# Interleaving two tensors: the opening half tile in four strided loads

## The chip, the cores and the metric

One Trainium2 chip, one core. The time is that of the device in microseconds, of one execution of the program; a kernel is run several times and the median is given. The profile is of one execution, and its span goes from the first to the last instruction.

## The reference

```python
def setup_inputs():
    batch, seq, dim = 32, 256, 1024
    return {
        "x": np.random.randn(batch, seq, dim).astype(np.float32),
        "y": np.random.randn(batch, seq, dim).astype(np.float32),
    }

def reference(x, y):
    result = np.zeros((batch, seq, dim * 2), dtype=np.float32)
    result[..., 0::2] = x
    result[..., 1::2] = y
```

Two fp32 tensors of 33.6 MB each are woven element by element into one of 67.1 MB. There is no arithmetic. 134.2 MB go through the core's transfers, half of it in and half of it out.

## The kernel before

Each input is taken as one flat row of numbers and cut into n = 8 tiles of 128 partitions x W = 8192 fp32 (4 MB, 32 KB a partition). There are two buffers each for x (`xt`), y (`yt`) and the output (`ot`). A tile of x and one of y give two output halves (h = 0, 1), each of 128 x 8192 elements: VectorE copies 4096 elements a partition of x into the even places of `ot[h]` (L70) and 4096 of y into the odd places (L73). So each output half is one transfer of 4 MB.

Three engines share the work, each with a program of its own, held together by semaphores alone:

- SP issues the loads. For each tile k it issues x (L55) and then y (L58). From tile 2 on it first waits on the semaphore `woven`, which VectorE raises after each copy, until the buffer is free. All of SP's transfers go through one queue.
- VectorE runs the copies in order: x into half 0, y into half 0, x into half 1, y into half 1. It waits for the x tile (`xsem`, L65), for the store that last used the output buffer (`osem`, L69), and for the y tile (`ysem`, L72).
- ACT issues the stores (L80) when `woven` says that a half is complete. The very first half is stored in two parts (2048 and 6144 columns). ACT's transfers go through a second queue.

The opening is special. The first x tile is loaded in two halves of 4096 columns: the first by SP (L46, `xsem[0]`), the second by ACT (L49, `hsem`). Between them in the program stands a tiny transfer of ACT (L48, `tsem`) that copies 16 x 128 elements from x to the output; the right values are stored over it later, and ACT waits for it before its first store. Every transfer raises its semaphore by 16 when it has landed, so a wait for one of them is a wait for 16.

A program begins with an opening block in which the engines meet at a barrier: each drains its work, signals, and goes on when all have. `tile_interleave_kernel` moves the first transfer of SP (L46) and the first of ACT (L48) out of the body and into that opening block, just ahead of each engine's drain, so that they are issued before the barrier (L101 to L119). All else, the second x half (L49) and the first y tile (L58) included, is issued after it.

Of the kernel before, what the change touches and what calls it, by code (L numbers as in the profile page):

```python
# [3 lines left out]


def _interleave(nc, x, y, out):
    P = 128
    W = 8192
    H = W // 2  # L10

    total = 1
    for s in x.shape:
        total *= s
    n = total // (P * W)
    assert n * P * W == total

    def rows(ap, names, k):
        flat = ap.rearrange("b s d -> (b s d)")
        return flat[k * names : (k + 1) * names].rearrange("(p w) -> p w", p=P)  # L20

    fp32 = mybir.dt.float32
    xt = [nc.alloc_sbuf_tensor(f"xt{b}", [P, W], fp32).ap() for b in (0, 1)]
    yt = [nc.alloc_sbuf_tensor(f"yt{b}", [P, W], fp32).ap() for b in (0, 1)]
    ot = [nc.alloc_sbuf_tensor(f"ot{b}", [P, W], fp32).ap() for b in (0, 1)]

    xsem = [nc.alloc_semaphore(f"xsem{b}") for b in (0, 1)]
    hsem = nc.alloc_semaphore("hsem")
    tsem = nc.alloc_semaphore("tsem")
    ysem = [nc.alloc_semaphore(f"ysem{b}") for b in (0, 1)]  # L30
    woven = nc.alloc_semaphore("woven")
    osem = [nc.alloc_semaphore(f"osem{b}") for b in (0, 1)]

    xs = [rows(x, P * W, k) for k in range(n)]
    ys = [rows(y, P * W, k) for k in range(n)]
    os_ = [rows(out, 2 * P * W, k) for k in range(n)]

    Q = W // 4

    def parts(k, h):  # L40
        return [slice(0, W)] if k or h else [slice(0, Q), slice(Q, W)]

    def stored(k, h):
        return 16 * sum(len(parts(j, h)) for j in range(k))

    nc.sync.dma_start(out=xt[0][:, :H], in_=xs[0][:, :H]).then_inc(xsem[0], 16)  # L46
    few = (slice(0, P, P // 16), slice(0, 128))
    nc.scalar.dma_start(out=os_[0][few], in_=xs[0][few]).then_inc(tsem, 16)  # L48
    nc.scalar.dma_start(out=xt[0][:, H:], in_=xs[0][:, H:]).then_inc(hsem, 16)  # L49
    for k in range(n):  # L50
        b = k % 2
        if k >= 2:
            nc.sync.wait_ge(woven, 4 * (k - 2) + 3)
        if k:
            nc.sync.dma_start(out=xt[b], in_=xs[k]).then_inc(xsem[b], 16)  # L55
        if k >= 2:
            nc.sync.wait_ge(woven, 4 * (k - 2) + 4)
        nc.sync.dma_start(out=yt[b], in_=ys[k]).then_inc(ysem[b], 16)  # L58

    for k in range(n):  # L60
        b = k % 2
        for h in (0, 1):
            c = slice(h * H, (h + 1) * H)
            if h == 0:
                nc.vector.wait_ge(xsem[b], 16 * (k // 2 + 1))  # L65
            elif k == 0:
                nc.vector.wait_ge(hsem, 16)
            if k:
                nc.vector.wait_ge(osem[h], stored(k, h))  # L69
            nc.vector.tensor_copy(out=ot[h][:, 0::2], in_=xt[b][:, c]).then_inc(woven, 1)  # L70
            if h == 0:
                nc.vector.wait_ge(ysem[b], 16 * (k // 2 + 1))  # L72
            nc.vector.tensor_copy(out=ot[h][:, 1::2], in_=yt[b][:, c]).then_inc(woven, 1)  # L73

    nc.scalar.wait_ge(tsem, 16)
    for k in range(n):
        for h in (0, 1):
            nc.scalar.wait_ge(woven, 4 * k + 2 * h + 2)
            for c in parts(k, h):
                nc.scalar.dma_start(  # L80
                    out=os_[k][:, h * W : (h + 1) * W][:, c], in_=ot[h][:, c]
                ).then_inc(osem[h], 16)

    nc.scalar.wait_ge(osem[0], stored(n, 0))
    used = sorted(s.num for s in [*xsem, hsem, tsem, *ysem, woven, osem[0]])
    assert used == list(range(used[0], used[-1] + 1)), used
    nc.scalar.sem_clear(range(used[0], used[-1] + 1))
    nc.sync.nop(nofuse=True).wait_op(osem[1], stored(n, 1), "sem-ge").then_inc(
        osem[1], -stored(n, 1)
    )  # L90


def kernel(tc, x, y, out):
    nc = tc.nc
    tc.close()
    tc.compile()

    _interleave(nc, x, y, out)

    blocks = nc.main_func.blocks  # L100
    for engine in (mybir.EngineType.SP, mybir.EngineType.Activation):  # L101
        opening = blocks[0].instructions
        at, moved = next(
            (b, i)
            for b in blocks[1:]
            for i in b.instructions
            if i.engine == engine and i.opcode == "DMACopy"
        )
        assert not (moved.sync_info and moved.sync_info.on_wait)
        body = at.instructions  # L110
        body.remove(moved)
        gate = next(
            n
            for n, i in enumerate(opening)
            if i.engine == engine and i.opcode == "Drain"
        )
        opening.insert(gate, moved)
        at.instructions = body
        blocks[0].instructions = opening  # L119


# [1 line left out]
_INS = ['x', 'y']  # L123
_OUTS = [((32, 256, 2048), 'float32')]


# [23 lines left out]
```

## Time and profile before

| what | value |
|---|---|
| median of 3 runs | 314.29 us (314.17 to 314.34) |
| profiled execution, its own time | 314.17 us |
| its span | 312.8 us |
| bytes read, written | 67.12 MB, 67.12 MB |
| VectorE busy | 72.0 us in 32 copies of 2.29 us |
| chain that ended last | DMA 82%, DVE 12% |

The chain that ended last is followed back from the last instruction; it says which work each step waited for. Here nearly all of it is transfers: VectorE's waits sum up to 206.4 us for stores to leave the output buffers, 11.1 us for the first y tile and 8.6 us for the first half of x. SP waited 217.9 us in six waits for buffers to come free. The issues and how long each took from issue to landing (columns: names, queue, kind, count, size of one, median us to landing):

```profile
out_dram<-ot ACTq DMA_DIRECT2D x15, 4096.0 KB, 34.1
yt<-in_y_dram SPq DMA_DIRECT2D x8, 4096.0 KB, 41.5
xt<-in_x_dram SPq DMA_DIRECT2D x7, 4096.0 KB, 24.3
out_dram<-ot ACTq DMA_DIRECT2D x1, 3072.0 KB, 32.7
xt<-in_x_dram SPq DMA_DIRECT2D x1, 2048.0 KB, 8.6
xt<-in_x_dram ACTq DMA_DIRECT2D x1, 2048.0 KB, 17.5
out_dram<-ot ACTq DMA_DIRECT2D x1, 1024.0 KB, 16.2
out_dram<-in_x_dram ACTq DMA_DIRECT2D x1, 8.0 KB, 6.0
```

A time to landing is long because transfers share the same 16 DMA engines and wait behind one another. 4 MB at the mean rate of 429 GB/s is 9.8 us of all 16 engines.

### The profile page before, as it was taken

Reading aid. Unit: us, or ns where it says so; the run is one execution under the profiler, and the core shown is the slowest. Engines: PE = TensorE matmul, PEld = TensorE weight load, DVE = VectorE, ACT = ScalarE, POOL = GpSimd, SP = SyncE. Lnnn points to the kernel's source line nnn. Section 1 sums busy time; section 2 is a strip of 40 time slices with the busy share of each in tenths; the row PEclk is TensorE's granted clock in tenths of the full one; section 3 lists DMA queues with packets and bytes.
Section 4 is the critical chain, followed back from the end, with each engine's and each line's share of the span. In section 5 each row is a group of like instructions: output and inputs, shape, how many; then the busy total and the mean of one; then the engine's idle time right before and its main releaser. Section 6 shows DMA issues by size and latency. Waiting matters only on the chain.

```text
span 312.8 us, 116 instructions
## 1 busy us (share of the span) xinstructions
DVE 72.0 (23%) x32; POOL 0.2 (0%) x4
## 2 busy tenths in 40 slices
DVE  0216000501405023050230503205032050415410
POOL 0000000000000000000000000000000000000000
DMA  8999999999999999999999999999999999999998
GB/s 336 436 436 436 436 402 432 440 457 415 448 423 427 444 402 469 402 469 402 469 402 465 406 448 423 427 444 402 469 402 469 402 469 402 465 406 448 423 432 373
DMA packets 4928, 134.23 MB, mean 429 GB/s; under 512 B 560, under 2 KB 576, under 8 KB 576
## 3 DMA queue, kind: packets, MB, share of 16 engines
q10 hardware_dynamic: 2624, 69.22, 51.3%
q1 hardware_dynamic: 2304, 65.01, 48.5%
HBM read 67.12 MB, written 67.12 MB: 429 GB/s over the span
## 4 chain that ended last, share of the span: by engine, by line
DMA 82%; DVE 12%; issue 0%
DMA out_dram<-ot 76%; DVE ot L73 6%; DMA yt<-in_y_dram 6%; DVE ot L70 6%
## 5 line engine op out<-in xcount | busy, mean ns | idle before, releaser
L70 DVE COPY ot<-xt 128x4096 f32<-128x4096 f32 x16 | 36.7, 2295 | 215.0 <-DMA out_dram<-ot 206.4
L73 DVE COPY ot<-yt 128x4096 f32<-128x4096 f32 x16 | 36.6, 2288 | 11.1 <-DMA yt<-in_y_dram 11.1
L134 POOL MEMSET const-bfloat16-1.0<- 128x1 bf16 x1 | 0.1, 101 | 0.0
L134 POOL MEMSET const-uint8-127<- 128x1 uint8 x1 | 0.1, 101 | 0.0
L134 POOL MEMSET const-float32-0.0<- 128x1 f32 x1 | 0.1, 98 | 0.2 <-issue 0.2
L134 POOL MEMSET const-float32-1.0<- 128x1 f32 x1 | 0.1, 98 | 0.0
## 6 DMA issues: line engine op xcount, KB each, us to landing
out_dram<-ot ACTq DMA_DIRECT2D x15, 4096.0 KB, 34.1
yt<-in_y_dram SPq DMA_DIRECT2D x8, 4096.0 KB, 41.5
xt<-in_x_dram SPq DMA_DIRECT2D x7, 4096.0 KB, 24.3
out_dram<-ot ACTq DMA_DIRECT2D x1, 3072.0 KB, 32.7
xt<-in_x_dram SPq DMA_DIRECT2D x1, 2048.0 KB, 8.6
xt<-in_x_dram ACTq DMA_DIRECT2D x1, 2048.0 KB, 17.5
out_dram<-ot ACTq DMA_DIRECT2D x1, 1024.0 KB, 16.2
out_dram<-in_x_dram ACTq DMA_DIRECT2D x1, 8.0 KB, 6.0
```

Source lines behind the costliest of these rows:

```text
L70: nc.vector.tensor_copy(out=ot[h][:, 0::2], in_=xt[b][:, c]).then_inc(woven, 1)
L73: nc.vector.tensor_copy(out=ot[h][:, 1::2], in_=yt[b][:, c]).then_inc(woven, 1)
L134: nc = _bacc.Bacc("TRN2", target_bir_lowering=False, num_devices=1)
```

## The change

The load of L46 becomes four loads of 32 rows each. The first takes partitions 0, 4, 8, ... 124, the second 1, 5, 9, ... and so on; the columns are the same 4096, so that each row is still one run of 16 KB in the source and in the buffer. The four raise the same semaphore, `xsem[0]`, by 16 each, and every wait of VectorE on `xsem[0]` is raised by 48 in turn. The code that moves instructions into the opening block now moves four transfers of SP and, as before, one of ACT. No other transfer, copy or buffer differs; SP has three more issues, all ahead of its drain.

```diff
+    R = 4
...
-    nc.sync.dma_start(out=xt[0][:, :H], in_=xs[0][:, :H]).then_inc(xsem[0], 16)
+    for r in range(R):
+        some = (slice(r, P, R), slice(0, H))
+        nc.sync.dma_start(out=xt[0][some], in_=xs[0][some]).then_inc(xsem[0], 16)
...
-                nc.vector.wait_ge(xsem[b], 16 * (k // 2 + 1))
+                nc.vector.wait_ge(xsem[b], 16 * (k // 2 + (1 if b else R)))
...
-    for engine in (mybir.EngineType.SP, mybir.EngineType.Activation):
-        opening = blocks[0].instructions
-        at, moved = next(
+    for engine, count in ((mybir.EngineType.SP, 4), (mybir.EngineType.Activation, 1)):
+        for _ in range(count):
+            opening = blocks[0].instructions
+            at, moved = next(
...
-        opening.insert(gate, moved)
-        at.instructions = body
-        blocks[0].instructions = opening
+            opening.insert(gate, moved)
+            at.instructions = body
+            blocks[0].instructions = opening
```

In the changed file the lines move: the four loads are L49, ACT's tiny transfer is L51, the second x half L52, the loads L58 and L61, the copies L73 and L76, the stores L83.

More of the change, by code (lines that the diff above doesn't have):

```diff
@@ L100 @@
     blocks = nc.main_func.blocks
-    for engine in (mybir.EngineType.SP, mybir.EngineType.Activation):
-        opening = blocks[0].instructions
-        at, moved = next(
[L104 to L116, printed above, removed]
-        opening.insert(gate, moved)
-        at.instructions = body
-        blocks[0].instructions = opening
+    for engine, count in ((mybir.EngineType.SP, 4), (mybir.EngineType.Activation, 1)):
+        for _ in range(count):
+            opening = blocks[0].instructions
+            at, moved = next(
+                (b, i)
+                for b in blocks[1:]
+                for i in b.instructions
+                if i.engine == engine and i.opcode == "DMACopy"
+            )
+            assert not (moved.sync_info and moved.sync_info.on_wait)
+            body = at.instructions
+            body.remove(moved)
+            gate = next(
+                n
+                for n, i in enumerate(opening)
+                if i.engine == engine and i.opcode == "Drain"
+            )
+            opening.insert(gate, moved)
+            at.instructions = body
+            blocks[0].instructions = opening
 _INS = ['x', 'y']
```

## The prediction

> **What bounds the kernel now.** I read the page first: span, busy shares, the forty slices.
>
> ```profile
> span 312.8 us, 116 instructions
> DVE 72.0 (23%) x32; POOL 0.2 (0%) x4
> DMA  8999999999999999999999999999999999999998
> GB/s 336 436 436 436 436 402 432 440 457 415 448 423 427 444 402 469 402 469 402 469 402 465 406 448 423 427 444 402 469 402 469 402 469 402 465 406 448 423 432 373
> DMA packets 4928, 134.23 MB, mean 429 GB/s; under 512 B 560, under 2 KB 576, under 8 KB 576
> ```
>
> The transfers are the bound: VectorE works 23% of the span, the DMA engines are at nine tenths or more in every slice but the first and last. Next the table by stretches, to see what the two ends cost (columns: stretch, length, DVE busy, POOL busy, clock, DMA share, GB/s).
>
> ```profile
> 0.00:1.00 1.00, 0.00 (x0) 0.20 (x4) 1.00 0.00 0
> 1.00:2.00 1.00, 0.00 (x0) 0.00 (x0) 1.00 1.11 279
> 2.00:3.00 1.00, 0.00 (x0) 0.00 (x0) 1.00 0.76 311
> 3.00:4.00 1.00, 0.00 (x0) 0.00 (x0) 1.00 1.08 459
> ...
> 40.00:140.00 100.00, 22.49 (x10) 0.00 (x0) 1.00 1.00 432
> 140.00:270.00 130.00, 26.98 (x12) 0.00 (x0) 1.00 1.01 434
> ```
>
> In the long middle the rate is (100 x 432 + 130 x 434) / 230 = 433 GB/s. All 134.23 MB at that rate take 310.0 us; 312.8 - 310.0 = 2.8 us is all that a better order of transfers can win. Of this, 1.0 us is the empty first microsecond. From 1 to 4 us 279 + 311 + 459 = 1,049 KB moved where 3 x 433 = 1,299 would have: 250 KB or 0.58 us of ramp. The other 1.2 us lie at the end, which the change doesn't touch. (A share of 1.11 shows that a packet counts where it starts, so a stretch this short is good to about one round of packets: 16 engines x 16 KB = 262 KB, 0.6 us.) Last the order of time at the opening, where the change lies.
>
> ```profile
> 0.00 0.36 SPq L46 DMA_DIRECT2D xt<-in_x_dram  x1
> 0.12 0.59 ACTq L48 DMA_DIRECT2D out_dram<-in_x_dram  x1
> ...
> 2.03 0.33 SPq L58 DMA_DIRECT2D yt<-in_y_dram  x1
> 2.03 0.36 ACTq L49 DMA_DIRECT2D xt<-in_x_dram  x1
> 2.41 0.43 SPq L55 DMA_DIRECT2D xt<-in_x_dram  x1
> 2.89 0.49 SPq L58 DMA_DIRECT2D yt<-in_y_dram  x1
> 8.60 2.30 DVE L70 COPY ot<-xt 128x4096 f32<-128x4096 f32 x1 [8.60 <-DMA xt<-in_x_dram]
> 21.96 2.29 DVE L73 COPY ot<-yt 128x4096 f32<-128x4096 f32 x1 [11.06 <-DMA yt<-in_y_dram]
> ```
>
> One load (L46) is issued at 0.00; its bytes begin to move a little after 1.0. The opening barrier lets SP and ACT go on at 2.03. VectorE's first copy starts at 8.60 and ends at 10.9; then it waits 11.06 us for the first y tile. So it isn't the landing of the opening half that sets anything, but how early all 16 DMA engines are streaming: what is lost there shifts everything behind it one for one.
>
> **The change, part by part.**
>
> *The load of L46 in four pieces.* The bytes and the 16 KB runs stay: 128 rows / 16 engines = 8 packets an engine, 16,384 B / (433 / 16 GB/s) = 0.605 us each, 4.84 us in all; now 2 packets an engine and piece. If a transfer's start-up grows with its rows, a quarter of the rows starts sooner, and the ramp of 0.58 us (up to 1.2 with the grain of the count) shrinks; if it is a fixed delay, nothing is gained. The rows lean to fixed: L48's transfer of 16 rows held ACT to 0.71, 0.35 after SP's 128 rows were done at 0.36, and that is no less than the 0.33 to 0.36 of 128 rows. Bounds: 0 to -1.2 us. I take -0.2, a third of the ramp counted.
>
> *Three more issues on SP.* Free-standing an issue takes 0.33 to 0.36 us (L58, L46), back to back 0.43 and 0.49. Four end at 0.36 + 3 x 0.33 = 1.35 at the least, at about 0.36 + 0.38 + 0.43 + 0.49 = 1.7, and at 1.83 with 0.49 each. An engine needs 2 x 0.605 = 1.21 us for its share of a piece and the next piece is issued 0.33 to 0.49 later, so no engine waits between pieces. Price 0.
>
> *The barrier comes later.* Today its last arrival is ACT's, whose issue ends at 0.71, and work goes on at 2.03, 1.32 later. With SP last, 1.35 to 1.83 + 1.32 = 2.7 to 3.15: up to 1.1 us later. Behind SP stand the y load (L58), the loads of tile 1 (L55, L58); behind ACT the second x half (L49). The cover is the opening half itself: it feeds the engines from about 1.0 to at least 5.8. With the 1.0 us that L46 shows from issue to movement, y is ready by 4.2, 1.6 us before it is needed. Price 0; if that cover were gone, each microsecond of lateness would cost one.
>
> *Three more completions.* 35 issues give 560 packets under 512 B, 16 each; now there are 48 more, 3 an engine. Slices 2 to 5 hold 436 GB/s although the ends of L46, L48, L49 and the first L58 lie in them; a stall of 0.1 us in every engine would take 1.3% (6 GB/s) off a 7.8 us slice. Bounds 0 to +0.3; I take 0.
>
> *The wait for 64 in place of 16* stands before VectorE's first copy, with the 11 us of idle behind it. Price 0; were that idle time gone, later landing would delay the first store.
>
> *Which rows a piece has.* Each piece writes every fourth partition. No transfer of this trace writes strided partitions, so it is unknown whether 16 engines can write such a piece at once as fast as 128 neighbouring rows. Bounds by the nearest rows: 0 at the full 0.605 us a packet, and, if two engines at a time share one way into the memory, twice that: 8 x 0.605 = +4.84 us. Taking 0 here is the choice on which the forecast hangs: the bytes, run lengths and packets are those of the 128-row rows, which are the only ones there are.
>
> [...]
>
> *Sum.* -0.2 + 0 + 0 + 0 + 0 + 0 = -0.2 us on the profiled execution: its own time is 314.17, 1.37 over its span of 312.8, so 313.97, span 312.6. The median of the three runs, 314.29, is 0.12 above; -0.2 from it gives 314.1.
>
> **The rivals.**
>
> *The strided pieces collide (slower).* Place: 1 to about 10 us, in the packets of the opening half alone; it decides as soon as a packet takes over 0.605 us for more than 0.8 us in sum over an engine's eight. All eight at half speed: +4.84, 319.1. Engines that start at different moments and packets of the second x half in between loosen it; with half the packets hit, +2.4, 316.7. I take the middle, +3.6: 317.9. For it: no strided write in the trace vouches for full speed, and the middle streams at a constant rate with engines at share 1.00, so an engine has nothing in reserve to make up for a shared way. Against it: all 16 engines have equal shares of each piece.
>
> *The whole start-up was the 128 rows (faster).* Ramp of 0.58 gone and the grain of the count in its favour, -0.6 to -1.2: 313.1 to 313.7, say 313.5. For it: 279 and 311 GB/s in the second and third microsecond, when a single transfer was in flight. Against it: the issue of 16 rows was no shorter than that of 128, and the pieces follow one another at 0.4 us, so the later rows still come later.
>
> *Seams (slightly slower).* Each of the three new seams stalls the engines for 0.3 us, more than the bound from the 436 GB/s slices; or y comes after the opening half is through: +0.9, 315.2. Against it the cover of 1.6 us and those slices.
>
> *That the pieces do nothing at all* (start-up fixed, seams free) gives 314.3; it ends as the forecast does and is counted with it.
>
> **How the numbers follow.** A measurement of this kernel can tell 0.2%, 0.63 us, from no change. Forecast (313.7 to 314.9, mostly 314.1): 0.46. Collision: 0.40. Whole ramp gained: 0.10. Seams: 0.04. Faster by over 0.2% needs more than the counted ramp, so it is the third alone: 0.10. Slower is collision and seams: 0.44. Same: 0.46. The predicted time is the forecast's, 314.1; its own range is 313.7 to 314.9. For 8 in 10 the range must take in most of the collision: up to 318.5 leaves out its upper quarter (0.10); down to 313.5 leaves out half of the third case (0.05).
>
> **What would show it.** In the stretches: 1 to 4 us moving more than 1,049 KB with the later total kept up to 10 us means the ramp shrank; the same 1,049, that it was fixed; a rate well under 433 from 3 to 8 us with the DMA share still at 1 means collision, and the middle unchanged at 433 in any case. In the order of time: four issues of L49 ending at 1.35 to 1.83, L61 and L52 at 2.7 to 3.15, first copy (L73) before 8.6 if the pieces run at full speed and after 9.5 if they collide, first copy from y (L76) near 21.8 by the forecast and near 25.5 by collision. The forecast is wrong if L76's first start moves by over 0.6 us either way, or if it stays and the span does not.

## The result and the profile after

The changed kernel takes 315.53 us (median of six runs, 315.29 to 316.48) against 314.26 (314.16 to 314.34) for the kernel before on the same chip: +1.27 us, ratio 1.0046, 95% interval 1.0035 to 1.0056. It is slower by more than the 0.2% that count here; no change was forecast, with 314.1 and a range of 313.7 to 314.9. The profiled execution took 315.56, span 314.2, which is 1.4 above the span of before.

The page of the changed kernel, first as a whole:

```profile
span 314.2 us, 119 instructions
...
GB/s 310 417 446 405 430 442 430 442 421 446 417 451 417 451 417 451 417 446 417 446 421 446 421 446 421 446 421 446 417 446 421 446 421 446 421 446 421 438 430 342
DMA packets 4977, 134.23 MB, mean 427 GB/s; under 512 B 609, under 2 KB 625, under 8 KB 625
```

The first two slices fall from 336 and 436 GB/s to 310 and 417; behind them the rate is what it was. The extra small packets are 49: 16 for each of the three added transfers and one of 32 bytes that is on neither SP's nor ACT's queue. Next the opening in order of time (start, length, queue or engine, line):

```profile
0.00 2.45 SPq L49 DMA_DIRECT2D xt<-in_x_dram  x4
0.12 0.59 ACTq L51 DMA_DIRECT2D out_dram<-in_x_dram  x1
...
3.75 0.34 SPq L61 DMA_DIRECT2D yt<-in_y_dram  x1
3.76 0.37 ACTq L52 DMA_DIRECT2D xt<-in_x_dram  x1
...
8.82 2.29 DVE L73 COPY ot<-xt 128x4096 f32<-128x4096 f32 x1 [8.82 <-DMA xt<-in_x_dram]
23.44 2.30 DVE L76 COPY ot<-yt 128x4096 f32<-128x4096 f32 x1 [12.32 <-DMA yt<-in_y_dram]
```

The four issues last to 2.45, not 1.35 to 1.83: one takes 0.55 to 0.59 us. So the barrier opens 1.72 later and y is issued at 3.75 in place of 2.03. The first copy from y starts at 23.44 in place of 21.96. This shift holds the whole loss of 1.4: everything behind is the old kernel, 1.3 to 1.8 us later copy by copy. The stretches of the changed kernel show where it arises (last column GB/s):

```profile
1.00:2.00 1.00, 0.00 (x0) 0.00 (x0) 1.00 1.16 262
2.00:3.00 1.00, 0.00 (x0) 0.00 (x0) 1.00 0.61 262
3.00:4.00 1.00, 0.00 (x0) 0.00 (x0) 1.00 1.08 451
4.00:6.00 2.00, 0.00 (x0) 0.00 (x0) 1.00 0.96 328
...
1.00:24.00 23.00, 2.86 (x2) 0.00 (x0) 1.00 1.00 408
...
40.00:270.00 230.00, 49.48 (x22) 0.00 (x0) 1.00 1.00 433
```

and the same of the kernel before:

```profile
4.00:6.00 2.00, 0.00 (x0) 0.00 (x0) 1.00 0.98 414
6.00:8.00 2.00, 0.00 (x0) 0.00 (x0) 1.00 1.05 451
...
1.00:24.00 23.00, 4.34 (x2) 0.00 (x0) 1.00 1.03 433
```

From 1 to 24 us 23 x (433 - 408) = 575 KB are missing, 1.3 us at 433 GB/s. The deepest hole is from 4 to 6 us, where the pieces are being moved: 328 in place of 414. The middle stays at 433. Note that the DMA share reads 0.96 there, with a packet of 1,608 ns (see the second chain below) counted as busy for all its time, so the share hides a hole that the rate shows.

The trace's packet records resolve it further. They don't name the DMA engine, but packets follow one another so closely (within 6 ns in the two chains below) that they can be chained by their times into 16 engines; where several end within a few ns of one another, the chain is a choice among them. Two chains of the changed kernel, each with the eight packets of an engine's share of the opening half (start + duration in ns from the span's start; all on SP's queue):

```
1337+1153 2487+611 3104+611 3711+611 4324+619 4939+620 5561+615 6172+1044
1358+1167 2522+611 3129+611 3736+611 4349+1608 5954+618 6574+611 7181+611
```

The packets of a strided piece take 611 ns, as those of the kernel before do; for 16 engines that is its mean rate (16 x 16,384 B / 611 ns = 429 GB/s). But behind the first sixteen, which take 744 to 1,522 ns, 18 of the 112 others are long, 756 to 1,704 ns. Seven of them start between 4.3 and 5.1 us, in the third piece, and eleven between 5.9 and 7.2, in the fourth; the chains above show one of each. Nothing makes up for it afterwards. In the kernel before, the 16 engines end their last packet between 312.18 and 312.46 us, in the changed one between 312.71 and 313.86. The program ends with the slowest of the sixteen (the span ends 0.4 us after the last packet in both kernels), so an engine's hole counts in full if it is the worst one.

### The profile page after: what moved, and what is told of

Read it like the earlier page. It is cut to its first block, busy times and chain, and to the rows that moved or that the text cites. A ratio compares the mean times of both kernels' runs of the same rounds, so it can differ in the third digit from the quotient of the medians.

```text
span 314.2 us, 119 instructions
## 1 busy us (share of the span) xinstructions
DVE 72.0 (23%) x32; POOL 0.2 (0%) x4
## 4 chain that ended last, share of the span: by engine, by line
DMA 82%; DVE 12%; issue 0%
DMA out_dram<-ot 76%; DVE ot L76 6%; DMA yt<-in_y_dram 6%; DVE ot L73 6%
## 5 line engine op out<-in xcount | busy, mean ns | idle before, releaser
L73 DVE COPY ot<-xt 128x4096 f32<-128x4096 f32 x16 | 36.7, 2295 | 215.1 <-DMA out_dram<-ot 206.3
L76 DVE COPY ot<-yt 128x4096 f32<-128x4096 f32 x16 | 36.6, 2290 | 12.3 <-DMA yt<-in_y_dram 12.3
```

## The experiments

Each is given against the kernel before on the same chip (314.25 to 314.28 there), with the ratio of the two and its 95% interval.

**1. The later barrier alone.** A VectorE memset holds the barrier back in the kernel before.

```diff
+    nc.vector.memset(ot[0][:, : 5 * W // 8], 0.0)   # e1; e5: [:, :1936]
...
+        mybir.EngineType.DVE: "Memset",             # moved ahead of DVE's drain
```

> The kernel before with one load of 128 rows, and a VectorE memset of 128 x 5120 ahead of VectorE's drain that holds the barrier back (the memset's area is overwritten later). The memset should take 2.5 to 5.3 us, so the first y issue moves from 2.03 to about 3.7 (as in the changed kernel, 3.75) or later. If the later barrier is what costs (the opening half runs out before y is there): +0.8 to +1.4 us against the kernel before. If the seams between pieces cost, or the placement of the strided rows: 0 +- 0.2 us, as long as y is issued by about 4.5.

> As the run with the memset ahead of the barrier, but with 128 x 1936: it should end at about 2.85 us, so that y is issued at about 3.75 as in the changed kernel, with one load of 128 rows on SP. Late barrier alone costs: +0.7 to +1.3 us against the kernel before. The pieces cost, or pieces and lateness together: 0 +- 0.2 us.

The first memset was too long. The order of time and the stretch behind it, of the run e1_late:

```profile
1.21 4.33 DVE L47 MEMSET ot<- 128x5120 f32 x1 [1.21 <-issue]
6.45 0.33 SPq L59 DMA_DIRECT2D yt<-in_y_dram  x1
```

```profile
6.00:8.00 2.00, 0.68 (x1) 0.00 (x0) 1.00 1.00 320
```

With y at 6.45 the engines run dry, the rate from 6 to 8 us is 320 in place of 451, and the kernel takes 315.78 us (1.0048, 1.0035 to 1.0061). That shows what the cover is worth when it is gone. With the shorter memset, y is issued at 3.13 and the time is 314.25 (0.9997, 0.9989 to 1.0006): 1.1 us of lateness cost nothing. 3.75 itself was not hit. In e1_late y's packets began 1.0 to 1.8 us after the issue, so y issued at 3.75 would be there by 5.6, and the opening half, alone on the engines there, is through at 6.5 to 7.0. That last step is worked out, not measured.

**2. Where the rows lie.** Pieces of neighbouring rows, and pieces of columns.

```diff
-        some = (slice(r, P, R), slice(0, H))
+        some = (slice(32 * r, 32 * r + 32), slice(0, H))                  # e2
+        some = (slice(0, P), slice(H // R * r, H // R * (r + 1)))         # e3
```

> The changed kernel with pieces of 32 neighbouring partitions in place of every fourth. If the seams or the late barrier cost: the same as the changed kernel, +1.1 to +1.5 us against the kernel before. If the placement of rows costs in the changed kernel: another time than that, 0 if neighbours don't collide, +2.4 to +4.9 if they collide more.

> The changed kernel with its four pieces cut by columns: 128 rows x 1024 columns each, so runs of 4 KB. Seams: +1.1 to +1.5 us, as there are as many pieces and each gives an engine the same bytes. Late barrier: +1.1 to +1.5 if the four issues again last to about 2.4 us, less if they are shorter. Placement: 0 +- 0.3, as all 128 rows are in each piece.

Neighbours: 318.72 us (1.0140, 1.0126 to 1.0154), +4.46. The stretches of e2_neighbours:

```profile
4.00:6.00 2.00, 0.00 (x0) 0.00 (x0) 1.00 1.01 213
6.00:8.00 2.00, 0.00 (x0) 0.00 (x0) 1.00 0.99 213
8.00:12.00 4.00, 0.00 (x0) 0.00 (x0) 1.00 0.99 221
```

The whole opening half runs at about half rate (213 to 221 GB/s), and its packets take 1.14 to 1.29 us. That is the factor of two that the prediction's rival had, but for 32 neighbouring rows; the packets of every fourth row don't have it (611 ns). What slows the neighbours was not shown. Pieces of neighbouring rows cost 3.2 us more than the rows that the change took (318.72 against 315.53).

Columns: 315.49 us (1.0038, 1.0025 to 1.0050), +1.23, as much as the changed kernel, with all 128 rows in each piece. But the equal time has no equal cause. The stretches of e3_columns have no such hole:

```profile
4.00:6.00 2.00, 0.00 (x0) 0.00 (x0) 1.00 1.02 410
...
1.00:24.00 23.00, 3.75 (x2) 0.00 (x0) 1.00 1.03 432
```

They are close to those of the kernel before (414 and 433). In this execution fifteen engines end between 312.35 and 312.77 us and one alone at 313.77; by the chained packets that one loses its time after 60 us. What did that is open. So this run doesn't tell whether the pieces' number or their rows cost in the changed kernel, and its 4 KB packets are slower by themselves too (159 ns for 4 KB, 25.8 GB/s an engine against 26.8 for 611 ns and 16 KB).

**3. Two queues in place of one.** The same four strided pieces, in turn on SP and ACT.

```diff
-        nc.sync.dma_start(out=xt[0][some], in_=xs[0][some]).then_inc(xsem[0], 16)
+        eng = nc.sync if r % 2 == 0 else nc.scalar
+        eng.dma_start(out=xt[0][some], in_=xs[0][some]).then_inc(xsem[0], 16)
...
-    for engine, count in ((mybir.EngineType.SP, 4), (mybir.EngineType.Activation, 1)):
+    for engine, count in ((mybir.EngineType.SP, 2), (mybir.EngineType.Activation, 2)):
```

> The four strided pieces of the changed kernel, pieces 0 and 2 issued by SP and 1 and 3 by ACT, all ahead of the barrier; ACT's tiny transfer comes after it. The issues should end at about 1.2 to 1.5 us in place of 2.45, and y be issued at about 2.5 to 2.9. Late barrier: most of the loss is gone, +0 to +0.4 us. Seams: the loss stays, +0.7 to +1.5. Placement: the loss stays, +1.1 to +1.5.

314.57 us (1.0011, 1.0002 to 1.0020), +0.31, and narrow: 314.49 to 314.82 in eleven runs. The stretches of e4_two_queues:

```profile
1.00:2.00 1.00, 0.00 (x0) 0.00 (x0) 1.00 1.14 229
...
4.00:6.00 2.00, 0.00 (x0) 0.00 (x0) 1.00 1.06 451
```

The hole from 4 to 6 us is gone, and behind an engine's second packet none of 16 KB takes over 0.69 us. What is left is the late start: the first packets begin at 1.32 us here and at 1.34 in the changed kernel, and at 1.0 with neighbouring rows, with columns and in the kernel before. So some 0.3 of the 1.27 us seem to belong to the strided shape, whose issue takes 0.55 us where 128 rows take 0.36, and 1.0 us to what the second queue removes. This run also has the barrier earlier (y at 2.76) and the tiny transfer behind it; the next runs separate these.

**4. y and the second half ahead of the barrier, and the tiny transfer behind it.**

```diff
-    for engine, count in ((mybir.EngineType.SP, 4), (mybir.EngineType.Activation, 1)):
+    for engine, count in ((mybir.EngineType.SP, 5), (mybir.EngineType.Activation, 2)):  # e6
+    for engine, count in ((mybir.EngineType.SP, 4),):                                   # e9
```

> The changed kernel with the first y load (SP, behind the four pieces) and the second x half (ACT) issued ahead of the barrier too: y at about 2.5 in place of 3.75, the half at about 0.75 in place of 3.76. Late barrier: what is left is the later first packet, +0.2 to +0.5 us against the kernel before. Seams of the pieces: +1.1 to +1.5 as in the changed kernel.

> The changed kernel with ACT's tiny transfer (16 x 128, from x to the output) issued after the barrier, ahead of the second x half, in place of ahead of the barrier; the four pieces stay on SP. If single DMA engines stall because short pieces follow one another on one queue: +0.9 to +1.5 us against the kernel before, as the changed kernel. If they stall because the tiny transfer falls between the pieces: +0.2 to +0.5, the later first packet alone.

Without the tiny transfer among the pieces: 315.67 us (1.0052, 1.0032 to 1.0073). The loss stays, so it isn't that; the rate from 4 to 6 us is 311 GB/s there. With y at 2.49 and the second half at 0.75: 315.32 (1.0033, 1.0016 to 1.0050). An earlier y alone doesn't take the loss away, but the twelve runs spread from 314.46 to 317.39, and five of them lie under 314.8. The execution that was profiled took 314.69, and in its packet records no engine stops: where the third piece's packets were missing, from 4.2 to 5.5 us, it took two or three packets of the second half from ACT's queue. In that execution the other queue's work filled the hole (410 GB/s from 4 to 6 us). Why other runs of this kernel took up to 2.7 us more was not seen, and stays open.

> The changed kernel once more, on the same chip as the other three: +1.0 to +1.4 us. Stalls at seams: the long packets of the opening half fall on other engines than in the first profile, behind the second and the last piece again. A fixed fault of placement: on the same rows again.

The changed kernel again: 315.45 us (1.0038, 1.0025 to 1.0051). In its profile the hole is there again (311 GB/s from 4 to 6 us), but twelve long packets start between 4.3 and 4.9 us, in the third piece, where the first profile had seven; a fault bound to certain rows would give the same each time.

**5. Controls on the kernel before.** y and the second half ahead of the barrier with one load (e7); the tiny transfer behind the barrier with one load (e11); two halves by columns, one on each queue (e8) or both on SP (e10).

> The kernel before with one load of 128 rows, and the first y load and the second x half issued ahead of the barrier: y at about 0.4. Both theories: 0 +- 0.2 us against the kernel before, since y is ahead of its need there already; if the kernel before already loses to lateness, faster by up to 0.5.

> The kernel before with its one load of 128 rows, and ACT's tiny transfer issued after the barrier. If the tiny transfer costs single engines the 0.1 to 0.3 us of idle time seen at 4.7 us in the kernel before: -0.1 to -0.3 us; otherwise 0 +- 0.1.

> The opening half as two loads of 128 rows x 2048 columns (runs of 8 KB), one by SP and one by ACT, both ahead of the barrier; ACT's tiny transfer comes after it. Barrier as early as before (y at about 2.1). Late barrier and seams both: 0 +- 0.3 us. If the slow start belongs to the time of one issue and its 128 rows: up to -0.4.

> The opening half as two loads of 128 rows x 2048 columns, both by SP ahead of the barrier; ACT's tiny transfer is ahead of it too. One seam in place of three, no strided rows, so the first packet at about 1.0 as before. Stalls at seams on one queue: +0.2 to +0.6 us, a third of the stalls. Strided or small pieces alone stall: 0 +- 0.2.

314.31 (1.0000, 0.9991 to 1.0009), 314.25 (1.0004, 0.9994 to 1.0015), 314.35 (1.0004, 0.9996 to 1.0013) and 314.23 us (0.9998, 0.9989 to 1.0006). None moves the time. So one seam on a queue (e10) costs nothing, which the theory of a price for each seam had at +0.2 to +0.6; and no version tried is faster than the kernel before. One of the eleven runs of e11 took 316.27.

**6. The third transfer of a queue.** A single seam being free, a new theory: an engine takes up the third transfer of one queue only when the first is done. The same bytes in two uneven loads or three, all on SP.

```diff
-        some = (slice(r, P, R), slice(0, H))
+    cuts = [0, 1024, 4096]        # e13, R = 2
+    cuts = [0, 512, 1024, 4096]   # e14, R = 3;  e17: [0, 3072, 3584, 4096]
+        some = (slice(0, P), slice(cuts[r], cuts[r + 1]))
```

> The opening half as two loads of all 128 rows on SP, of 1024 and 3072 columns, both ahead of the barrier. Theory A (an engine takes up a third transfer of one queue only when the first of them is done, so that short transfers leave it without work): only two are there ahead of y, so 0 +- 0.2 us against the kernel before. Theory B (each seam on one queue costs): +0.2 to +0.5.

> The same bytes, but the first 1024 columns as two loads of 512, so three loads of 128 rows on SP: 512, 512, 3072 columns. Theory A: the third can't be taken up before the first is done at about 2.5 us, and the engines have about 1.3 us of work by then: idle time of 0.3 to 1 us in single engines between 2.5 and 4.5 us, +0.4 to +1.0 us. Theory B: two seams, +0.4 to +0.8. Neither: 0 +- 0.2.

Three: 317.54 us (1.0105, 1.0083 to 1.0127), +3.3, far more than expected. The stretches of e14_three_uneven:

```profile
3.00:4.00 1.00, 0.00 (x0) 0.00 (x0) 1.00 0.52 111
4.00:6.00 2.00, 0.00 (x0) 0.00 (x0) 1.00 0.83 283
```

The two short loads are through by about 2.9 us; then most engines stand without work, and the long third, issued by 1.48, delivers its first packets between 3.6 and 6 us. Two loads: 315.05 us (1.0028, 1.0014 to 1.0042), where 0 was expected. Four of the twelve runs lie at 314.20 to 314.32, as the theory has it, the others up to 316.50. In the profiled execution (315.11) fifteen engines end at 312.34 to 312.67 and one alone at 313.40; that one was no further behind than the rest at 32 us and lost 0.8 us between 32 and 100 us, after the opening. What did that is open; it isn't the opening's hole.

Then the same three loads, with the third on ACT, and in the other order.

```diff
+        eng = nc.sync if r < 2 else nc.scalar     # e16, cuts as in e14
```

> The three uneven loads (512, 512, 3072 columns, +3.3 us with all three on SP), the third issued by ACT ahead of the barrier and ACT's tiny transfer after it. Same loads, same runs. Theory A (the third of a queue is taken up only when the first is done): no queue has three, so the loss goes, 0 to +0.4 us, and no stretch from 2 to 6 us under 350 GB/s. If the short loads cost by themselves: +2 us or more.

> The three uneven loads on SP in the other order: 3072, 512, 512 columns. Theory A: the third has to wait for the first again, but that is done at about 5 us, when the second x half of ACT's queue has work for the engines, so most of the hole is covered: 0 to +0.6 us. If three loads on one queue cost in any order: +2 us or more.

314.46 us (1.0005, 0.9997 to 1.0014) with the third on the other queue (and the tiny transfer behind the barrier, which e9 and e11 show to be free): of +3.3 us +0.2 are left. The stretches of e16_three_third_on_act:

```profile
3.00:4.00 1.00, 0.00 (x0) 0.00 (x0) 1.00 0.97 393
4.00:6.00 2.00, 0.00 (x0) 0.00 (x0) 1.00 1.00 381
```

In the other order on SP: 314.50 (1.0016, 1.0006 to 1.0026), 314.20 to 315.93. So with these loads the short ones cost little by themselves (+0.2), and so do three on a queue where the first is long (+0.25); what costs is a third transfer behind two short ones on one queue. Short is here 8 packets of 84 ns an engine. The four columns of e3 set a limit to the rule: the first two loads there give an engine 8 x 159 ns = 1.27 us of work each, and the third follows without a hole, but for some 0.5 us in two engines.

> The four pieces of 128 rows x 1024 columns, in turn on SP and ACT as in the run with two queues, ACT's tiny transfer after the barrier. On one queue they cost +1.2 us. Theory A: two on each queue, none waits, so the loss goes: +0 to +0.3 us (what the 4 KB runs cost in rate). Theory B: as many seams but each covered by the other queue: the same. If the columns lose by something else (short runs): still +0.8 or more.

The four columns on two queues: 314.95 us (1.0022, 1.0013 to 1.0030) against 315.49 on one. About half of their loss is gone, less than expected. As e3 had no hole in its opening, a second queue had none to fill; in this execution too one engine ends alone, at 313.05 us, the others by 312.71. What the columns lose by is open.

## Why the prediction was wrong

**The step that failed** is in "Three more issues on SP": "An engine needs 2 x 0.605 = 1.21 us for its share of a piece and the next piece is issued 0.33 to 0.49 later, so no engine waits between pieces. Price 0." It took an issued piece for one that an engine can work on. The runs showed about 1.0 us in its place (+1.27 with four pieces on one queue, +0.31 with two on each of two): pieces one and two run through, and then engines stop in the third piece or the fourth. In the second chain shown above the fourth packet ends at 4.35 us, 2.5 us after the issue of the third piece ended at 1.82 by the instruction records, and the fifth, which needs 0.61 us, is through only at 5.96. The argument from the 436 GB/s slices did not reach this case: the transfers whose ends lie there are 8 packets an engine long, and the other queue had work (the end of L48, at 6.1 us, lies in the first slice and not in these).

Why the engines stop is known in part. That it hangs on the queue is shown: the same strided pieces on two queues have no hole (451 GB/s from 4 to 6 us, where one queue had 328). That a transfer waits until the last but one on its queue is complete fits e14, e16 and e17; in the changed kernel the first piece has landed at 3.9 us and the first packets of the third start at 4.3. But no row shows the wait itself, it says nothing of the long packets that are the last of the fourth piece, and by e3 four loads of 1.27 us an engine on one queue have almost no hole, where these pieces of 1.21 have one. What else the strided pieces bring, the longer issues or two packets an engine in place of eight, was not separated; four strided pieces with a long first one, for example, were not run.

**The length of an issue** was mis-sized as well: 0.55 to 0.59 us, not 0.33 to 0.49. The row for it was there. L48 took 0.59 us for 16 rows with a step, and the prediction read that as 0.35 behind SP's issue; but in the changed kernel SP's first issue lasts to 0.55 and ACT's tiny transfer still ends its issue at 0.71, so the 0.59 are its own.

**The gain of -0.2** for a shorter start-up was a loss of about 0.3: the rows leant to "fixed", and the first packet came at 1.34 in place of 1.02, most likely for the longer strided issue (0.55 us in place of 0.36). The engines did start closer together, the first packets at 1.34 to 1.72 against 1.02 to 1.99; it bought nothing.

**The barrier** was right in mechanism (last arrival on SP, 1.30 us from the end of the issues to y), wrong in size (3.75 against 2.7 to 3.15) by the issues' length. Its price of 0 holds up to 3.13, by measurement.

**The completions and the wait for 64** were rightly near nothing: e4_two_queues has the same completions and loses 0.31 in all, and the first copy of the changed kernel started at 8.82, with 12.3 us of idle time behind it.

**The rows of a piece**: the forecast hung on 0 for them, and for the rate of a packet that held, 611 ns. The doubled packet time that took 0.40 of the chance came with neighbouring rows (1.14 to 1.29 us a packet, and +4.46 us, where +4.84 had been worked out for it). That two engines share one way into the memory, which the prediction supposed for it, is shown by no run.

**The rivals.** The one that came nearest was the seams, 315.2 at a chance of 0.04. It was dismissed with rows that had long transfers on both queues. That the wider range for 8 in 10, 313.5 to 318.5, holds the measured time is luck: it was stretched for the collision, which did not happen. The prediction's own sign came true: L76's first start moved by 1.48 us, over the 0.6 that it had named. The sum of terms was also made for an average engine, where the end is set by the worst of sixteen: in the changed kernel the best engine ends 0.5 us later than the best one before, the worst 1.4 later than the worst.

## What to carry to other kernels

A transfer that has been issued was not yet work for the engines here: with several short transfers on one queue, a later one came late although it was issued in time (in e14 issued by 1.48 us, first packets from 3.6). Spreading the short pieces over two queues took most of that away here (+1.27 to +0.31, +3.3 to +0.2), and so did a long first one (+3.3 to +0.25). When cutting a load by rows, spread the rows over the partitions (every fourth: 611 ns a packet; 32 neighbours: 1.14 to 1.29 us). In a kernel bound by transfers look at the rate in GB/s, not the DMA share (328 in place of 414 GB/s here, at 0.96 in place of 0.98), and at the slowest engine, not the mean.

## What was not expected of the hardware

An engine's hole in the opening is still there 300 us later: the spread of their last packets was 0.28 us before and 1.15 after. Chained to the end, every engine of the kernel before moves the same 8,192 KB, a sixteenth; nothing there shows one taking over work from another. A strided issue of 32 rows holds SP for 0.55 to 0.59 us, one of 32 neighbours for 0.38 to 0.62 (median 0.41), one of 128 rows for 0.36. And some kernels with several short loads scatter by 2 to 3 us from run to run (e6, e9, e13, e14) where the kernel before keeps within 0.6, but for one run of 35 at 315.12; the profile of a single execution can't tell why, and e11, with its one load, had a run at 316.27 too.
